# Evacuation adds in place, masks in the pooling stage, the two-quarter chunk's down groups whole, and quarter 7 of FFN 0 by eight products

## The chip, the cores and the metric

The kernel runs on one core of one Trainium2 chip. TensorE (PE) multiplies into PSUM; its weight loads are shown apart as PEld. VectorE (DVE) and ScalarE (ACT) do the elementwise work, GpSimd (POOL) and SyncE (SP) mostly issue transfers. The metric is the device time of one execution in microseconds, as the median of the runs.

## The reference

A trunk of two layers over 256 tokens of width 2048. Layer 0 mixes by causal pooling, layer 1 by dilated attention; each is followed by a gated feed-forward part (FFN) with a causal convolution of width 3, and each of the four sums is normalised. The FFN is where the change acts most:

```python
def conv_ffn(h, w_up, conv_w, conv_b, w_down):
    S = h.shape[1]
    u = h @ w_up
    up = jnp.pad(u, ((0, 0), (CONV_WIDTH - 1, 0), (0, 0)))
    c = conv_b + up[:, 0:S] * conv_w[0]
    for j in range(1, CONV_WIDTH):
        c = c + up[:, j:j + S] * conv_w[j]
    gate, val = jnp.split(c, 2, axis=-1)
    return (jax.nn.silu(gate) * val) @ w_down
...
        h = layer_norm(DEEPNORM_ALPHA * h + mix, ln1_g[i], ln1_b[i])
        ff = conv_ffn(h, ffn_w_up[i], ffn_conv_w[i], ffn_conv_b[i], ffn_w_down[i])
        h = layer_norm(DEEPNORM_ALPHA * h + ff, ln2_g[i], ln2_b[i])
```

The inner width is 5504 = 43 blocks of 128. In attention the scores are masked by which of the three dilated branches see a pair of positions, and weighted by how many do.

## The kernel before

Every weight is float32 and is multiplied as two float32r parts, a rounded high part (`wh`, cast by ScalarE) and the rest (`wl`, subtracted by VectorE), so that a product is three matmuls: high by high, low by high, high by low.

The program is one list of **units**. A unit is a block of weights of up to 512 x 512 with its load into a raw buffer (three in rotation, on SP's queue), its split into `wh` and `wl` (four in rotation), its matmuls, and what follows them. `run_units` writes them out in order: before unit i it issues loads up to unit i + 5 and splits up to unit i + 3, and behind its matmuls come the callbacks due (`later(n, fn)`: n units on), then the unit's own evacuation. Every engine works in the order written.

An FFN runs in eleven **quarters** of 512 inner columns (the last has three blocks, 384). `up(q)` gives quarter q's four gate units and four value units, 32 matmul steps each (24 in the last); their sums are evacuated (`evac`) from PSUM into a tile `u`, convolved (`conv`), and multiplied to `g`. The down product of the inner quarters is done in four **chunks**, of quarters 0 to 2, 3 to 5, 6 and 7, and 8 to 10. For each chunk `down(n)` gives four groups, one for each 512 output columns, of one item for each quarter. An item is either a plain unit (`go_t`: 24 matmuls of 512 columns, which is eight half-size products) or a **7-product** pair of units (`mk_seven`, kinds "a" and "b": 18 and 24 matmuls of 256 columns, seven half-size products). The latter needs sums and differences of the weights, formed in the raw buffer itself by `split_sums` (three VectorE steps more than a plain split, with the raw buffer held until kind "b" is split), and of the tokens, formed by `left_sums` when the quarter's `g` is ready, in borrowed buffers named by `sets`. `sevens` says which quarters do which column groups so. A group's sums lie in four PSUM banks (`t0`, `t1`, `s2`, `s3`); `early_post` and `tm_post` add them to the token-major residual `HT`, three transfers by POOL among them. In FFN 0 the third chunk is the last by tokens: three units behind each of its groups, `to_features` turns that residual back to feature-major by a VectorE transpose and 16 moves on SP's queue.

The groups of one chunk are laid among the up units of the next quarters by `weave`. With three items to a group there is one item behind each up unit but the first; with two items there is one before the first and one before the third up unit. Quarter 9's `g` is made only behind the last group of the two-quarter chunk (`free[9]`), since it takes a buffer that the group still reads; in FFN 1 its 7-product operands follow.

`evac` copies the second half of a PSUM bank with ScalarE to a tile of a ring of three (`ut`), and VectorE adds the first half to it into `u`; attention's `qk_post` does the same with a ring of two, `norm_evac` works likewise for the first group of a stage. The two mask tiles (`cnt`, `negm`) are made at the start of attention by `masks`, in that same ring.

Of the kernel before, what the change touches and what calls it, by code (L numbers as in the profile page):

```python
# [17 lines left out]
T = 256  # L18
# [14 lines left out]
def trunk(ctx: ExitStack, tc: tile.TileContext, x, pool_w_in, pool_w_grp, pool_scale, pool_w_out,  # L33
# [269 lines left out]
    inv = const.tile([P, 1, 16], F32, name="inv")  # L303

# [134 lines left out]
    def norm_evac(ps, nb, tmp, dst):  # L439
# [108 lines left out]
    def ffn(lay):  # L548
# [17 lines left out]
        def evac(ps, nb, mode):  # L566
            fp = pools["ffn"]
            u = pads()

            def tmp():  # L570
                return fp.tile([P, T], F32, name="ut", tag="t1", bufs=3)

            if mode == "x":
                norm_evac(ps, nb, tmp, lambda m: u[:, m, 2:])
                return u
            for m in range(nb):
                t = tmp()
                A.copy(t, ps[m][:, T:])  # L578
                V.tensor_tensor(u[:, m, 2:], ps[m][:, :T], t, OP.add)  # L579
# [155 lines left out]
        def down(n, last):  # L735
            qs = range(*chunks[n])
# [224 lines left out]
    def qk_post(nm, hq):  # L961
# [3 lines left out]
        def evac(ps):  # L965
# [4 lines left out]
            def tmp():  # L970
                return ap.tile([P, T], F32, name="qt", tag="t1", bufs=2)

            if hq == 0 and nm == "k":
                norm_evac(ps, 4, tmp, lambda m: o[:, m, :])
# [13 lines left out]
    def scores(hq, ms):  # L988
        ap = pools["attn"]
        for m in ms:  # L990
# [7 lines left out]
            sf, nf, cf = (t.rearrange("p a b -> p (a b)") for t in (s, ST["negm"], ST["cnt"]))  # L998
# [9 lines left out]
        for m in ms:  # L1008
            s, mx, _ = pr[hq, m]
            sf, cf = (t.rearrange("p a b -> p (a b)") for t in (s, ST["cnt"]))  # L1010
# [101 lines left out]
    with tc.tile_pool(name="pool", bufs=1) as pp:  # L1112
# [36 lines left out]

        later(2, lambda: late_consts(0))  # L1150
# [7 lines left out]
    with tc.tile_pool(name="attn", bufs=1) as ap:  # L1158
        pools["attn"] = ap
        for nm in ("cnt", "negm"):  # L1160
            ST[nm] = ap.tile([P, 3, P], F32, name=nm)

        def masks(i):
            two = ap.tile([P, 2, P], F32, name="dist", tag="t1", bufs=2)
# [54 lines left out]
```

## Time and profile before

| | us |
|---|---|
| median of 3 runs (lowest, highest) | 2051.32 (2048.59, 2051.43) |
| the profiled execution | 2051.56 |
| its span | 2049.8 |
| FFN 0, third chunk with the up groups of quarters 9 and 10 | 745.4 to 870.8 |
| FFN 0, last chunk begins | 870.8 |
| attention begins | 938.8 |
| FFN 1, third chunk with the up groups of quarters 9 and 10 | 1853.0 to 1974.1 |
| FFN 1, last chunk begins | 1974.1 |

Times in the views are microseconds from the span's start. A row of the waits reads: engine, tile and line that waited, the releaser, the total, the number of times, the longest. A row of the stretches reads: the stretch, its length, then for PE, PEld, DVE, ACT and POOL the busy time with the number of instructions, then the granted clock of PE, the share of DMA time and GB/s. In a timeline row stand the start, the length, engine, line and operation, and in brackets the idle time before it with its releaser.

### The profile page before, as it was taken

Reading aid. Unit: us, or ns where it says so; the run is one execution under the profiler, and the core shown is the slowest. Engines: PE = TensorE matmul, PEld = TensorE weight load, DVE = VectorE, ACT = ScalarE, POOL = GpSimd, SP = SyncE. Lnnn points to the kernel's source line nnn. Section 1 sums busy time; section 2 is a strip of 40 time slices with the busy share of each in tenths; the row PEclk is TensorE's granted clock in tenths of the full one; section 3 lists DMA queues with packets and bytes.
Section 4 is the critical chain, followed back from the end, with each engine's and each line's share of the span. In section 5 each row is a group of like instructions: output and inputs, shape, how many; then the busy total and the mean of one; then the engine's idle time right before and its main releaser. Section 6 shows DMA issues by size and latency. Waiting matters only on the chain. (4 is left out here: it accounts for less than half of the span.)

```text
span 2049.8 us, 31251 instructions
## 1 busy us (share of the span) xinstructions
PE 2025.5 (99%) x12532; PEld 1809.4 (88%) x12532; DVE 1684.2 (82%) x2010; ACT 1259.6 (61%) x1691; POOL 74.9 (4%) x111
## 2 busy tenths in 40 slices
PE   9999999999999999999999999999999999999998
PEld 8899988899899989889888888998899988889987
DVE  6759876998889898889856657787889888989989
ACT  6545687666756686657544444477666677667663
POOL 2000000000000101000000000000001000100000
PEclk9999999999999999999999999999999999999999
DMA  8655467667656657775566554557666756666565
GB/s 263 213 190 186 169 211 202 191 194 235 196 190 201 202 190 210 211 231 170 167 218 191 173 180 165 185 185 221 187 199 185 227 181 208 205 216 197 184 206 185
DMA packets 278305, 405.92 MB, mean 198 GB/s; under 512 B 80414, under 2 KB 95668, under 8 KB 277904
## 3 DMA queue, kind: packets, MB, share of 16 engines
q1 hardware_dynamic: 266144, 389.72, 57.5%
q0 software_dynamic: 11584, 13.55, 4.4%
q8 instruction: 98, 1.61, 0.3%
q10 hardware_dynamic: 432, 0.66, 0.1%
q14 instruction: 47, 0.39, 0.1%
HBM read 380.01 MB, written 2.10 MB: 186 GB/s over the span
## 5 line engine op out<-in xcount | busy, mean ns | idle before, releaser
L165 PE MATMUL acc<-xc,wh 128*128 128x512 f32 x3264 | 1152.8, 396 | 1.2 <-DVE o L1064 1.2
L166 PE MATMUL acc<-xc,wl 128*128 128x256 f32 x3264 | 917.3, 281 | 5.3 <-DVE wl L83 5.1
L83 DVE TENSOR_TENSOR wl<-raw,wh 128x2048 fp32r<-128x2048 f32 (+2 forms) x318 | 687.5, 2168 | 259.1 <-ACT wh L82 258.7
L165 PEld LDWEIGHTS acc<-xc,wh 128*128 128x128 f32 x3264 | 615.9, 189 | 144.4 <-DVE o L1064 1.9
L82 ACT CAST wh<-raw 128x2048 fp32r<-128x2048 f32 (+2 forms) x318 | 573.7, 1810 | 201.2 <-PE acc L165 108.4
L166 PEld LDWEIGHTS acc<-xc,wl 128*128 128x128 f32 x3264 | 615.4, 189 | 9.2 <-DVE wl L83 8.5
L96 ACT CAST wh<-raw 128x1024 fp32r<-128x1024 f32 x116 | 121.9, 1053 | 156.8 <-DVE raw L107 133.4
L97 DVE TENSOR_TENSOR wl<-raw,wh 128x1024 fp32r<-128x1024 f32 x116 | 138.4, 1221 | 0.0
L103 ACT CAST wh<-raw 128x1024 fp32r<-128x1024 f32 x116 | 90.7, 832 | 35.6 <-DMA raw<-in_ffn_w_down_dram 21.3
L106 DVE TENSOR_TENSOR wl<-raw,wh 128x1024 fp32r<-128x1024 f32 x116 | 105.7, 952 | 2.6 <-ACT wh L103 2.2
L587 ACT ACTIVATE c<-u,cv 128x256 f32<-128x256 f32 x172 | 89.5, 593 | 24.6 <-DVE f L650 8.5
L578 ACT COPY ut<-acc 128x256 f32<-128x256 f32 x164 | 53.1, 372 | 81.6 <-DVE u L579 58.6
L228 PE MATMUL t<-wl,g 128*128 128x256 f32 x344 | 97.0, 282 | 0.0
L227 PE MATMUL t<-wh,g 128*128 128x256 f32 x344 | 97.0, 282 | 0.0
L229 PE MATMUL t<-wh,g 128*128 128x256 f32 x344 | 96.7, 281 | 0.0
L228 PE MATMUL s<-wl,xs 128*128 128x256 f32 x308 | 86.9, 282 | 3.8 <-DVE wl L97 3.8
L229 PE MATMUL s<-wh,xs 128*128 128x256 f32 x308 | 86.4, 280 | 0.0
L227 PE MATMUL s<-wh,xs 128*128 128x256 f32 x308 | 86.3, 280 | 0.0
L271 POOL DMA_DIRECT2D ht<-w x24 | 20.3, 847 | 1770.6 <-ACT wh L103 1034.8
L592 ACT ACTIVATE a<-u,cv 128x256 f32<-128x256 f32 x172 | 73.6, 501 | 12.3 <-DVE g L660 6.5
L592 ACT ACTIVATE u<-u,cv 128x256 f32<-128x256 f32 x172 | 73.5, 500 | 0.0
L109 DVE TENSOR_TENSOR raw<-raw 128x1024 f32<-128x1024 f32 x58 | 71.0, 1225 | 2.0
(278 smaller groups left out, 3433.8 us busy)
## 6 DMA issues: line engine op xcount, KB each, us to landing
raw<-in_ffn_w_up_dram SPq DMA_DIRECT2D x160, 1024.0 KB, 4.9
raw<-in_ffn_w_down_dram SPq DMA_DIRECT2D x80, 1024.0 KB, 5.1
raw<-in_pool_w_out_dram SPq DMA_DIRECT2D x16, 1024.0 KB, 5.0
raw<-in_shared_w_k_dram SPq DMA_DIRECT2D x16, 1024.0 KB, 5.1
raw<-in_attn_w_q_dram SPq DMA_DIRECT2D x16, 1024.0 KB, 5.4
raw<-in_shared_w_v_dram SPq DMA_DIRECT2D x16, 1024.0 KB, 5.6
raw<-in_attn_w_o_dram SPq DMA_DIRECT2D x16, 1024.0 KB, 5.0
raw<-in_pool_w_in_dram SPq DMA_DIRECT2D x12, 1024.0 KB, 5.5
```

Of the source, the lines that this page charges most:

```text
L82: A.copy(wh[i][:, s], r[:, s])
L83: V.tensor_tensor(wl[i][:, s], r[:, s], wh[i][:, s].bitcast(F32), OP.subtract)
L96: A.copy(h[:, :, n], r[:, :, n])
L97: V.tensor_tensor(l[:, :, n], r[:, :, n], h[:, :, n].bitcast(F32), OP.subtract)
L103: A.copy(h[:, k, n], r[:, k, n])
L106: V.tensor_tensor(l[:, k, n], r[:, k, n], h[:, k, n].bitcast(F32), OP.subtract)
L165: PE.matmul(ps[m], h[:, k, c], q[:, k, :, :T], start=st, stop=False)
L166: PE.matmul(ps[m][:, :T], l[:, k, c], q[:, k, 0, :T], start=False, stop=sp and not shifted)
L227: PE.matmul(to, xh, h[:, k, n], start=opens and kk == 0, stop=False)
L228: PE.matmul(to, xh, l[:, k, n], start=False, stop=False)
L229: PE.matmul(to, xl, h[:, k, n], start=False, stop=ends and kk == 1)
L592: A.activation(to[:, m, :], u[:, m, i:i + T], AF.Copy, scale=cv[:, i, j:j + 1])
```

## The change

It has four parts.

- Evacuation: ScalarE copies straight into the target tile, and VectorE adds the other half of the bank onto it there. The rings `ut` and `qt` are gone, in `evac`, `qk_post` and `norm_evac`.
- Masks: `cnt` and `negm` become constants of the whole program and are made in the pooling stage, behind units 11 and 12, in buffers that the normalisation uses later.
- Two-quarter chunk, both FFNs: a group's items stand together, behind a whole up group.
- FFN 0, quarter 7: plain units in place of 7-product pairs, in the order 7, 6; it has no left sums.

```diff
+    cnt = const.tile([P, 3, P], F32, name="cnt")
+    negm = const.tile([P, 3, P], F32, name="negm")
...
-    def norm_evac(ps, nb, tmp, dst):
+    def norm_evac(ps, nb, dst):
...
-            ts = [(m, tmp()) for m in range(m0, min(nb, m0 + 2))]
+            ts = [(m, dst(m)) for m in range(m0, min(nb, m0 + 2))]
...
-                A.activation(dst(m), t, AF.Identity, scale=-1.0, bias=wgb[:, m, 1:2])
+                A.activation(t, t, AF.Identity, scale=-1.0, bias=wgb[:, m, 1:2])
...
-        sets = {0: "C", 1: "A", 2: "B", 3: "C", 4: "A", 5: "B", 6: "A", 7: "BC"[1 - lay], 9: "A"}
+        sets = {0: "C", 1: "A", 2: "B", 3: "C", 4: "A", 5: "B", 6: "A", 7: "B", 9: "A"}
         if lay == 1:
             sevens[9] = (0, 2)
+        else:
+            del sevens[7]
...
             for m in range(nb):
-                t = tmp()
-                A.copy(t, ps[m][:, T:])
-                V.tensor_tensor(u[:, m, 2:], ps[m][:, :T], t, OP.add)
+                A.copy(u[:, m, 2:], ps[m][:, T:])
+                V.tensor_tensor(u[:, m, 2:], u[:, m, 2:], ps[m][:, :T], OP.add)
...
-            qs = range(*chunks[n])
+            qs = (7, 6) if n == 2 and lay == 0 else range(*chunks[n])
...
         d = down(2, False)
-        for us in up(8):
+        for us, ks in zip(up(8) + up(9) + up(10), [()] + d + [()]):
             units.extend(us)
-        for us, ks in zip(up(9) + up(10), d):
-            free[9] = weave(us, ks)[-1]
+            units.extend(ks)
+        free[9] = len(units) - 5
...
             for m in range(4):
-                    t = tmp()
-                    A.copy(t, ps[m][:, T:])
-                    V.tensor_tensor(o[:, m, :], ps[m][:, :T], t, OP.add)
+                    A.copy(o[:, m, :], ps[m][:, T:])
+                    V.tensor_tensor(o[:, m, :], o[:, m, :], ps[m][:, :T], OP.add)
...
         def masks(i):
-            two = ap.tile([P, 2, P], F32, name="dist", tag="t1", bufs=2)
-            dist, fm = two[:, 0], two[:, 1]
+            both = lnp.tile([P, 4, T], F32, name="dist", tag="sq")
+            dist, fm = (both[:, j, :P] for j in range(2))
+            two = lnp.tile([P, 2, T], I32, name="idist", tag="fold2")
+            idist, im = two[:, 0, :P], two[:, 1, :P]
...
         for i in range(2):
-            later(7 + i, lambda i=i: masks(i))
+            later(9 + i, lambda i=i: masks(i))
```

The order of the loads shows the new place of the groups. On SP's queue, in FFN 1, the last two groups of the two-quarter chunk before (`raw400` is the number of the unit that the load serves; down loads are the pairs, up loads of 384 columns belong to quarter 10):

```order
L72 DMA raw396_18240<-in_ffn_w_down_dram 128x4x512
L72 DMA raw398_18323<-in_ffn_w_up_dram 128x4x384
L72 DMA raw399_18364<-in_ffn_w_up_dram 128x4x384
L72 DMA raw400_18405<-in_ffn_w_down_dram 128x4x512
L72 DMA raw402_18457<-in_ffn_w_up_dram 128x4x384
L72 DMA raw403_18505<-in_ffn_w_up_dram 128x4x384
L72 DMA raw404_18537<-in_ffn_w_down_dram 128x4x512
L72 DMA raw406_18608<-in_ffn_w_up_dram 128x4x384
L72 DMA raw407_18648<-in_ffn_w_up_dram 128x4x384
L72 DMA raw408_18687<-in_ffn_w_down_dram 128x4x512
```

The same place of the changed program:

```order
L72 DMA raw394_18003<-in_ffn_w_up_dram 128x4x384
L72 DMA raw395_18039<-in_ffn_w_up_dram 128x4x384
L72 DMA raw396_18069<-in_ffn_w_down_dram 128x4x512
L72 DMA raw398_18143<-in_ffn_w_down_dram 128x4x512
L72 DMA raw400_18208<-in_ffn_w_up_dram 128x4x384
L72 DMA raw401_18251<-in_ffn_w_up_dram 128x4x384
L72 DMA raw402_18285<-in_ffn_w_up_dram 128x4x384
L72 DMA raw403_18320<-in_ffn_w_up_dram 128x4x384
L72 DMA raw404_18348<-in_ffn_w_down_dram 128x4x512
```

Before, every third load is a down load, three loads behind the one before it; now two stand together, then four up loads, and `raw404` already belongs to the last chunk, with two more up units between it and the last pair.

The same queue in FFN 0, before, with the moves of `to_features` (`h<-hb`):

```order
L72 DMA raw172_7917<-in_ffn_w_down_dram 128x4x512
L72 DMA raw174_8002<-in_ffn_w_up_dram 128x4x384
L804 DMA h_8037<-hb_7995 32x8x32 x6
L72 DMA raw175_8050<-in_ffn_w_up_dram 128x4x384
L804 DMA h_8037<-hb_7995 32x8x32 x5
L72 DMA raw176_8096<-in_ffn_w_down_dram 128x4x512
L804 DMA h_8037<-hb_7995 32x8x32 x5
L72 DMA raw178_8153<-in_ffn_w_up_dram 128x4x384
```

And in the changed program, where `raw173` is quarter 7's plain unit and `raw174` quarter 6's pair:

```order
L72 DMA raw169_7755<-in_ffn_w_up_dram 128x4x384
L72 DMA raw170_7800<-in_ffn_w_up_dram 128x4x384
L803 DMA h_7840<-hb_7798 32x8x32 x6
L72 DMA raw171_7857<-in_ffn_w_up_dram 128x4x384
L803 DMA h_7840<-hb_7798 32x8x32 x5
L72 DMA raw172_7901<-in_ffn_w_up_dram 128x4x384
L803 DMA h_7840<-hb_7798 32x8x32 x5
L72 DMA raw173_7936<-in_ffn_w_down_dram 128x4x512
L72 DMA raw174_7985<-in_ffn_w_down_dram 128x4x512
```

The moves stood around the second down load of a pair; now they stand among the group's last two up loads and ahead of the next group's plain load.

The third place is VectorE at the end of FFN 1's third chunk. Before, quarter 9's low part (`g`) and its left sums (`f`) come behind the split of `wl408`, the first unit of the last chunk:

```order
L83 TENSOR_TENSOR wl407_18721<-raw407_18648,wh407_18720 128x1536
L83 TENSOR_TENSOR wl408_18743<-raw408_18687,wh408_18742 128x2048
L286 TENSOR_TENSOR g_18770<-c_17996,g_18770 128x4x256
L646 TENSOR_TENSOR f_18777<-c_17996 128x256
L647 TENSOR_TENSOR f_18777<-f_18777,c_17996 128x256
L648 TENSOR_TENSOR f_18777<-c_17996 128x256
L650 TENSOR_TENSOR f_18777<-c_17996,f_18777 128x256
```

In the changed program they come behind the third of the last four up units, `wl402`; the first unit of the last chunk is now 404:

```order
L592 TENSOR_TENSOR c_18281<-c_18281,u_18243 128x768
L83 TENSOR_TENSOR wl402_18351<-raw402_18285,wh402_18350 128x1536
L286 TENSOR_TENSOR g_18378<-c_17680,g_18378 128x4x256
L645 TENSOR_TENSOR f_18385<-c_17680 128x256
L646 TENSOR_TENSOR f_18385<-f_18385,c_17680 128x256
L647 TENSOR_TENSOR f_18385<-c_17680 128x256
L649 TENSOR_TENSOR f_18385<-c_17680,f_18385 128x256
```

Two splits of short up units, 403 and with it the unit before the last chunk's first, have moved from ahead of quarter 9's operands to behind them.

More of the change, by code (lines that the diff above doesn't have):

```diff
@@ L997, in scores @@
             s = two[:, m % 2]
-            sf, nf, cf = (t.rearrange("p a b -> p (a b)") for t in (s, ST["negm"], ST["cnt"]))
+            sf, nf, cf = (t.rearrange("p a b -> p (a b)") for t in (s, negm, cnt))
             V.scalar_tensor_tensor(sf, ps[:, :3 * P], scale, nf, op0=OP.mult, op1=OP.add)
@@ L1009, in scores @@
             s, mx, _ = pr[hq, m]
-            sf, cf = (t.rearrange("p a b -> p (a b)") for t in (s, ST["cnt"]))
+            sf, cf = (t.rearrange("p a b -> p (a b)") for t in (s, cnt))
             for t, sl in parts:
```

45 lines of the change are left out of this document (18 added, 27 removed).

## The prediction

> **What bounds the kernel now.** The first view is the page: it says which engine is full.
>
> ```profile
> span 2049.8 us, 31251 instructions
> PE 2025.5 (99%) x12532; PEld 1809.4 (88%) x12532; DVE 1684.2 (82%) x2010; ACT 1259.6 (61%) x1691; POOL 74.9 (4%) x111
> ```
>
> TensorE is busy 99% of the span, so a change can only pay by issuing fewer matmuls or by taking away the few places where PE waits. The second view is the list of PE's waits, which names the releasers.
>
> ```profile
> PE acc L166 <- DVE wl L83: 5.1, 8, 2.0
> PE s L228 <- DVE wl L97: 3.8, 4, 1.5
> PE t L229 <- DVE xs3Q L660: 1.9, 1, 1.9
> ...
> PE acc L165 <- DVE o L1064: 1.2, 1, 1.2
> PE acc L165 <- DVE w L829: 1.1, 1, 1.1
> ...
> PE acc L165 <- DVE u L835: 0.7, 1, 0.7
> ```
>
> All of these wait for VectorE. The sums are too small, though: the end of a matmul is modelled, the records overlap, and the head of every stall hides behind the matmul before it. The third view therefore compares stretches that issue the same matmuls. The bounds of each are starts of units; the count in brackets includes the matmuls that overlap an edge.
>
> ```profile
> 745.45:778.46 33.01, 32.64 (x215) 29.50 (x213) 31.38 (x34) 25.86 (x36) 0.78 (x2) 1.00 0.57 191
> 810.84:841.22 30.38, 27.29 (x182) 24.66 (x181) 27.74 (x33) 18.85 (x30) 2.58 (x3) 1.00 0.77 208
> 841.22:870.78 29.56, 27.59 (x182) 24.72 (x181) 22.71 (x24) 17.87 (x25) 2.59 (x3) 1.00 0.75 210
> 870.78:879.15 8.37, 6.53 (x34) 4.94 (x33) 8.23 (x12) 4.43 (x5) 2.58 (x3) 1.00 0.81 228
> 879.15:884.80 5.65, 5.65 (x35) 4.92 (x34) 3.18 (x6) 5.30 (x10) 0.00 (x0) 1.00 1.02 333
> 1853.03:1885.75 32.72, 32.68 (x215) 29.56 (x213) 31.09 (x34) 25.58 (x36) 0.76 (x2) 1.00 0.56 193
> 1885.75:1918.15 32.40, 32.40 (x215) 29.55 (x213) 30.14 (x34) 22.12 (x31) 4.41 (x6) 1.00 0.68 203
> 1918.15:1945.04 26.89, 26.89 (x183) 24.65 (x182) 23.36 (x28) 17.39 (x26) 0.00 (x0) 1.00 0.65 207
> 1945.04:1974.10 29.06, 27.68 (x183) 24.77 (x181) 23.48 (x25) 19.25 (x26) 2.59 (x3) 1.00 0.70 219
> 1974.10:1988.92 14.82, 12.61 (x69) 11.14 (x67) 14.60 (x25) 8.84 (x16) 2.58 (x3) 0.88 0.50 126
> 2008.42:2018.96 10.54, 10.54 (x68) 9.49 (x66) 10.40 (x13) 6.20 (x5) 0.00 (x0) 1.00 0.34 108
> ```
>
> A group of the two-quarter chunk with three-block up units (two pairs of 7-product units and four up units, 180 matmuls) takes 26.89 us when nothing is late. In FFN 0 the two such groups take 30.38 and 29.56, a loss of 3.49 + 2.67 = 6.2 us, and the first group of full up units takes 33.01 where 32.40 is the calm length, 0.6. The first unit of the last FFN 0 chunk takes 8.37 where its twin takes 5.65: 2.7 us. In FFN 1 the groups lose 0.32 + 2.17 = 2.5 us, and the opening of its last chunk (a plain unit and a 7-product pair, 66 matmuls) takes 14.82 against 10.54: 4.3 us. Together **16.3 us** of stalls in the stages whose order is changed.
>
> Why the groups stall is read from the VectorE timeline of the late FFN 1 group and from the load queue.
>
> ```profile
> 1948.57 0.37 SPq L72 DMA_DIRECT2D raw<-in_ffn_w_down_dram  x1
> ...
> 1955.15 0.69 DVE L104 TENSOR_TENSOR raw<-raw 128x512 f32<-128x512 f32 x1 [2.26 <-DMA raw<-in_ffn_w_down_dram]
> 1956.24 1.83 DVE L106 TENSOR_TENSOR wl<-raw,wh 128x1024 fp32r<-128x1024 f32 x2 [0.40 <-ACT wh L103]
> 1958.10 0.69 DVE L107 TENSOR_TENSOR raw<-raw 128x512 f32<-128x512 f32 x1
> 1958.83 1.22 DVE L109 TENSOR_TENSOR raw<-raw 128x1024 f32<-128x1024 f32 x1
> 1959.97 0.95 DVE L593 TENSOR_TENSOR c<-c,a 128x768 f32<-128x768 f32 x1
> 1960.84 2.35 DVE L97 TENSOR_TENSOR wl<-raw,wh 128x1024 fp32r<-128x1024 f32 x2
> ...
> 1963.98 1.75 DVE L83 TENSOR_TENSOR wl<-raw,wh 128x1536 fp32r<-128x1536 f32 x1
> ...
> SPq L72 <- DVE wl L97: 421.1, 54, 10.2
> ```
>
> The load of the second pair's weights leaves at 1948.57, VectorE idles 2.26 us for it at 1955, and the pair's second half is split only from 1960.84, when PE is at that unit. The load left late because there are three raw buffers and the woven order is 7-product, up, up: each 7-product load takes the buffer of the 7-product load before it, which is held through all five split steps (L104 to L97). The queue's own waits say so: 54 loads waited for an L97. VectorE is not short of time here (23.48 us busy of 29.06); it is late.
>
> **The change, part by part.**
>
> *Eight products in place of seven.* A plain unit is 24 matmuls of 512 columns, a 7-product pair 42 of 256:
>
> ```profile
> 1974.10:1979.68 5.58, 5.58 (x27) 4.52 (x26) 5.42 (x12) 1.24 (x3) 1.70 (x3) 1.00 0.44 144
> 1853.03:1857.99 4.96, 4.96 (x44) 4.96 (x43) 4.96 (x7) 4.07 (x8) 0.00 (x0) 1.00 0.55 194
> ```
>
> 5.58 - 4.96 = 0.62 us of PE per column group, four groups: **+2.5 us**, on the engine that sets the end. VectorE gets back 0.69 + 1.83 + 0.69 + 1.22 + 2.35 = 6.8 us per pair and pays 2.3 for a plain split (the 512-column form of the 1.75 us row above), plus 0.3 for a full-width add of t1: some 4 us per group, 16 in all, and the left sums of quarter 7 fall away.
>
> *Groups whole.* With loads in the order 7, 6, up, up, up, up (6 then 7 in FFN 1) the three buffers turn differently: the first load of a group takes the buffer of the second of the four up units before it, and the second that of the third, both freed after one short split. A buffer held by a 7-product pair now goes to the second or third up unit behind it, which has slack. Walked through for the tightest place, the last group of FFN 1, from the start of up group 10's gate units (PE: short up unit (26.89 - 2 x 4.96) / 4 = 4.24, so 17.0; the group 9.9, to 26.9; four up units, to 43.9; plain unit, to 49.4). A split can start three units ahead of its unit, when PE frees the weight buffer. Split 7a may start at 12.7 and ends at 17.1; the evacuation of the gate ends at 18.3; split 7b ends at 20.6 and PE wants it at 24.1. Then three up splits of 1.75 (two convolution adds of 0.95 between them), quarter 9's four left sums and its low part (2.6 by the rows below), the group's own evacuation (2.6) and the fourth up split end near 34.4, wanted at 39.6. The plain split ends near 38, the two halves of quarter 9's pair near 42.4 and 44.7, wanted at 49.4 and 51.5. The smallest slack is 3.5 us, and no PE wait is left. In FFN 0 the group owes VectorE 4 us less.
>
> *The opening of the last chunk.* In FFN 1 quarter 9's own operands are made only behind the last group, which now ends four up units before the chunk in place of two:
>
> ```profile
> 1970.33 2.29 DVE L83 TENSOR_TENSOR wl<-raw,wh 128x2048 fp32r<-128x2048 f32 x1 [2.24 <-ACT wh L82]
> 1972.54 1.22 DVE L286 TENSOR_TENSOR g<-c,g 128x1024 fp32r<-128x1024 f32 x1
> 1973.68 0.42 DVE L646 TENSOR_TENSOR f<-c 128x256 f32<-128x256 f32 x1
> ...
> 1982.96 0.42 DVE L660 TENSOR_TENSOR xs3Q<-f,xs3S 128x256 fp32r<-128x256 f32 x1
> ```
>
> They are begun at 1972.5 and end at 1983.4, while PE waits. Two up units more are 8.5 us of PE time ahead of them, against a wait of 4.3. In FFN 0 the same shift frees the product banks that the 8.37 us unit waits for (L829 and L835 in PE's waits). What becomes late next is quarter 10's value chain, which still starts at the last up unit.
>
> ```profile
> 1983.10 0.91 ACT L578 COPY ut<-acc 128x256 f32<-128x256 f32 x3
> ...
> 1991.05 0.96 DVE L684 TENSOR_TENSOR c<-c 128x768 f32<-128x768 f32 x1
> ```
>
> In FFN 1 its copies began at 1983.10 and its product ended at 1992.0; with the cast and the low part behind that, my estimate is 13 us, and it has 49.4 + 4.96 + 5.6 - 43.9 = 16.
>
> *What follows each group.* The 16 small moves of FFN 0's turn to features keep their number and stand between other loads:
>
> ```profile
> 852.46 3.87 SPq L804 DMA_DIRECT2D h<-hb  x6
> ```
>
> 0.65 us of queue each, 10.3 per group. They now stand ahead of the last two up loads and the next plain load, whose splits have over 5 us in the walk. I charge nothing; if that cover is gone, one load is late by up to 3.9 us per group.
>
> *Evacuation in place and masks.* The copy loses its ring of three:
>
> ```profile
> ACT ut L578 <- DVE u L579: 58.6, 27, 3.8
> ...
> L1176 DVE SCALAR_TENSOR_TENSOR cnt<-dist,cnt x4: 292/293/295, 987.9 to 995.4; 128x128 f32<-128x128 f32 x4
> 82.78 2.29 DVE L83 TENSOR_TENSOR wl<-raw,wh 128x2048 fp32r<-128x2048 f32 x1 [3.28 <-ACT wh L82]
> ```
>
> ScalarE loses 58.6 us of waiting, but it is 61% busy and PE's waits name it nowhere in these stages. The add keeps its form and time. Two of the 164 copies now begin with a wait on VectorE for the buffer of u itself; behind it stand weight casts with three units of lead. The masks are ten VectorE steps of 0.22 to 0.29 us, 2.4 us twice. They move into the pooling stage, where VectorE idles 3.28 us before the split at 82.78; without that cover they would cost 2.4 us each. In the attention stage they ended 40 us before PE's one wait there (o L1064, 1.2 us), so between 0 and 1.2 is gained. I take zero for both edits, with -1.2 to +2.4.
>
> **The sum.** Of 16.3 us I let a fifth stay (3.3), because the walk leaves out loads that land late and ScalarE's share: 13.0 gained, 2.5 paid, 10.5 net. The profiled execution took 2051.56 (span 2049.8 and 1.8 around it), 0.24 above the median of the three runs, so 2051.56 - 10.5 = 2041.1. All stalls gone gives 2037.8, half of them 2045.9.
>
> **The rivals.**
>
> *The loads are the limit.* In FFN 0 the late groups moved 208 and 210 GB/s; to take 27.5 us in place of 30 they need 230. Against it: one unit moved 333. If so, the two groups stay at 30 us and absorb their own share of the price (1.2), and only four fifths of 0.6 + 2.7 + 2.5 + 4.3 are gained: 2051.6 - 8.1 + 1.2 = 2044.7.
>
> *Only FFN 0 gains.* If VectorE is simply full in FFN 1 (31.09 of 32.72 us in one group), its 6.8 us stay and four fifths of FFN 0's 9.5 go: 2051.6 - 7.6 + 2.5 = 2046.5.
>
> *The burst starves PE (slower).* In FFN 1 the two 7-product pairs now stand back to back: 2 x 6.8 = 13.6 us of VectorE for 9.9 us of PE, 3.7 us short. The walk covers it with 3.5 us of slack; if VectorE comes later than the walk by more than that, each further microsecond is PE's, in four groups. With the whole shortage paid, 4 x 3.7 = 14.8 in place of 2.5, the tail unchanged, FFN 0 as forecast: 2051.6 + 2.5 - 7.6 + 12.3 = 2059; half the shortage gives 2051. The Trainium skill (Perfetto Trace Analysis, Optimization Strategy) says that regimes bound by different engines may gain from being interleaved; the change takes interleaving away, so that rule stands on this rival's side. The trace so far speaks against it: the interleaved order is the one that stalls.
>
> *The waits move and only the price counts (slower).* PE is at 99%, the work of VectorE in FFN 1 is the same, and a wait removed may come back three units later: 2051.6 + 2.5 = 2054. The Trainium skill (Perfetto Trace Analysis, Identifying the Most-Contended Engine) has one improve the engine with the highest occupancy first; here that is PE, and the change adds to it. Against it stands the calm group of 26.89 us with 3.5 us of VectorE idle.
>
> **How the numbers follow.** The forecast of 2041 gets 0.68, the load limit 0.14, gain in FFN 0 alone 0.07, the burst 0.06, the price alone 0.05. The range runs from 2037 (all stalls gone, and most of the attention wait) to 2047.5 (the first two rivals); outside are the slower cases and their neighbours. A difference of 0.2%, 4.1 us, is about what this measurement can tell from none: faster means under 2047.2. Nearly all of the forecast, the load limit and half of FFN 0 alone lie there: 0.84. Within 0.2%: 0.09, the rest of these and the milder ends of the slower rivals. Slower: 0.07.
>
> **What would show it.** Right: groups of FFN 1 at 26.9 and 32.4 us, those of FFN 0 at about 33.0 and 27.5; the opening of FFN 1's last chunk near 10.6; PE's wait for xs3Q gone; the load queue's wait for L97 far under 421 us. Wrong: stalls at the second pair of FFN 1's groups (the burst), VectorE idle for loads in FFN 0 with DMA shares of 0.8 or more (the load limit), a new wait at quarter 10's first use, or 7-product loads that still land less than three units ahead.

## The result, and the profile after

| | before | changed |
|---|---|---|
| median, us | 2051.32 | 2030.07 |
| lowest, highest (5 runs each) | 2048.59, 2053.28 | 2029.58, 2031.27 |
| profiled execution, its span | 2051.56, 2049.8 | 2031.27, 2029.5 |

The ratio is 0.9899 with an interval of 0.9885 to 0.9914: the change takes 21 us, twice the 10.5 that were forecast, and the time lies below the range. The page of the changed kernel, its first lines:

```profile
span 2029.5 us, 31025 instructions
...
PE 2021.9 (100%) x12460; PEld 1807.1 (89%) x12460; DVE 1664.9 (82%) x1979; ACT 1253.3 (62%) x1676; POOL 75.0 (4%) x111
```

And the whole list of PE's waits of half a microsecond and more:

```profile
PE acc L168 <- ACT wh L82: 1.3, 1, 1.3
PE warm L1093 <- DVE one L1089: 1.1, 1, 1.1
PE xT L518 <- DMA xin<-in_x_dram: 0.9, 1, 0.9
```

PE's busy time fell by only 3.6 us and its idle time from 24.3 to 7.6. Every wait that the prediction showed is gone; the three that are left end within the first 10 us, up to the matmuls of the first unit. The stretches that answer to those of before, again bounded by unit starts:

```profile
636.60:744.83 108.23, 108.23 (x703) 98.19 (x702) 97.96 (x106) 72.98 (x98) 5.17 (x6) 1.00 0.69 218
744.83:865.59 120.76, 120.76 (x715) 106.50 (x714) 95.96 (x97) 74.76 (x98) 10.36 (x12) 1.00 0.76 220
777.83:810.83 33.00, 33.00 (x197) 29.07 (x196) 25.61 (x26) 20.60 (x27) 2.59 (x3) 1.00 0.77 210
838.21:865.59 27.38, 27.38 (x165) 24.18 (x164) 20.75 (x22) 15.92 (x19) 2.59 (x3) 1.00 0.87 247
865.59:871.21 5.62, 5.62 (x35) 4.91 (x34) 3.29 (x5) 3.61 (x6) 0.00 (x0) 1.00 0.67 193
1873.77:1906.16 32.39, 32.39 (x215) 29.55 (x214) 30.14 (x36) 22.25 (x30) 2.59 (x3) 1.00 0.67 209
1932.95:1959.74 26.79, 26.79 (x183) 24.63 (x182) 25.82 (x35) 18.48 (x25) 2.59 (x3) 1.00 0.72 223
1959.74:1970.30 10.56, 10.56 (x69) 9.47 (x68) 9.47 (x12) 9.77 (x16) 0.00 (x0) 1.00 0.65 225
```

Where the second number equals the first, PE had no gap at all. That now holds in every row: the groups of FFN 1 take 32.39 and 26.79, those of FFN 0 33.00 and 27.38 (0.6 more, the eight products' price), and the openings of the last chunks 5.62 and 10.56 against 8.37 and 14.82. The first row is a stretch that the prediction never looked at, the second chunk of FFN 0, with three items to a group. Before, the same 703 matmuls took longer:

```profile
635.29:745.45 110.16, 109.13 (x703) 98.25 (x702) 97.61 (x109) 70.11 (x96) 6.75 (x8) 1.00 0.65 206
```

Neither its order nor its products were changed, yet it is 1.9 us shorter and without a gap. That points at the evacuation, which the experiments take by itself.

### The profile page after: what moved, and what is told of

The parts are those of the page before. It is cut to its first block, busy times and chain, and to the rows that moved or that the text cites. A ratio compares the mean times of both kernels' runs of the same rounds, so it can differ in the third digit from the quotient of the medians.

```text
span 2029.5 us, 31025 instructions
## 1 busy us (share of the span) xinstructions
PE 2021.9 (100%) x12460; PEld 1807.1 (89%) x12460; DVE 1664.9 (82%) x1979; ACT 1253.3 (62%) x1676; POOL 75.0 (4%) x111
## 4 chain that ended last, share of the span: by engine, by line
PE 99%; DMA 0%; SPq 0%; DVE 0%; ACT 0%; issue 0%; DVEq 0%
PE acc L165 43%; PE acc L166 22%; PE t L238 3%; PE t L240 3%; PE t L239 3%; PE acc L169 3%; PE acc L170 3%; PE acc L168 3%; PE s L228 3%; PE s L227 2%; PE s L229 2%; PE t L228 2%; PE t L227 2%; PE t L229 2%; PE s L989 0%; PE o L1056 0%
## 5 line engine op out<-in xcount | busy, mean ns | idle before, releaser
L83 DVE TENSOR_TENSOR wl<-raw,wh 128x2048 fp32r<-128x2048 f32 (+2 forms) x322 | 697.0, 2169 | 251.7 <-ACT wh L82 248.6
L82 ACT CAST wh<-raw 128x2048 fp32r<-128x2048 f32 (+2 forms) x322 | 582.0, 1812 | 221.4 <-PE acc L165 120.3
L96 ACT CAST wh<-raw 128x1024 fp32r<-128x1024 f32 x108 | 112.9, 1053 | 149.0 <-DVE raw L107 123.1
L97 DVE TENSOR_TENSOR wl<-raw,wh 128x1024 fp32r<-128x1024 f32 x108 | 129.1, 1221 | 1.4 <-ACT wh L96 1.4
L103 ACT CAST wh<-raw 128x1024 fp32r<-128x1024 f32 x108 | 84.5, 832 | 48.5 <-PE acc L165 33.8
L106 DVE TENSOR_TENSOR wl<-raw,wh 128x1024 fp32r<-128x1024 f32 x108 | 98.3, 951 | 1.7 <-ACT wh L103 1.4
L228 PE MATMUL t<-wl,g 128*128 128x256 f32 x320 | 89.8, 281 | 0.0
L227 PE MATMUL t<-wh,g 128*128 128x256 f32 x320 | 89.8, 281 | 0.0
L229 PE MATMUL t<-wh,g 128*128 128x256 f32 x320 | 89.7, 280 | 0.0
L271 POOL DMA_DIRECT2D ht<-w x24 | 20.3, 847 | 1809.2 <-ACT wh L103 771.9
L577 ACT COPY u<-acc 128x256 f32<-128x256 f32 x164 | 54.7, 373 | 51.5 <-PE acc L166 51.4
L229 PE MATMUL s<-wh,xs 128*128 128x256 f32 x284 | 79.2, 279 | 0.0
L228 PE MATMUL s<-wl,xs 128*128 128x256 f32 x284 | 79.2, 279 | 0.0
L227 PE MATMUL s<-wh,xs 128*128 128x256 f32 x284 | 79.2, 279 | 0.0
L238 PE MATMUL t<-wh,g 128*128 128x512 f32 (+1 forms) x179 | 68.2, 381 | 0.0
```

Of the source, the lines that this page charges most:

```text
L82: A.copy(wh[i][:, s], r[:, s])
L83: V.tensor_tensor(wl[i][:, s], r[:, s], wh[i][:, s].bitcast(F32), OP.subtract)
L96: A.copy(h[:, :, n], r[:, :, n])
L97: V.tensor_tensor(l[:, :, n], r[:, :, n], h[:, :, n].bitcast(F32), OP.subtract)
L106: V.tensor_tensor(l[:, k, n], r[:, k, n], h[:, k, n].bitcast(F32), OP.subtract)
L227: PE.matmul(to, xh, h[:, k, n], start=opens and kk == 0, stop=False)
```

## The experiments

In each run one part is done alone, left out, or replaced. A diff is against the kernel before, unless another is named.

**The parts alone.** The evacuation in place, everywhere:

```diff
...
-                t = tmp()
-                A.copy(t, ps[m][:, T:])
-                V.tensor_tensor(u[:, m, 2:], ps[m][:, :T], t, OP.add)
+                A.copy(u[:, m, 2:], ps[m][:, T:])
+                V.tensor_tensor(u[:, m, 2:], u[:, m, 2:], ps[m][:, :T], OP.add)
...
```

> Before with the in-place evacuation alone (FFN, attention, norm). Theory A (ring): in the ring of three, ScalarE's fourth copy waits for VectorE's first add, a weight cast stands behind that copy, and VectorE then idles for that cast; without the ring the stalls of the three-quarter chunk (1.9 us in FFN 0, 1.3 in FFN 1) and of attention (1.2) go, and some of the two-quarter chunk's: 5 to 9 us less than before, 2042 to 2046. Theory B (as forecast): ScalarE's waits hide nothing, 2050 to 2052, and those 4.5 us come from the new order of the groups.

2038.93 us, ratio 0.9936 (0.9923 to 0.9948): 13 us, more than any other part alone, and 3 us below the numbers of theory A, which had the mechanism but gave it too little.

The groups whole, with seven products and the old ring:

```diff
-        for us in up(8):
+        for us, ks in zip(up(8) + up(9) + up(10), [()] + d + [()]):
             units.extend(us)
-        for us, ks in zip(up(9) + up(10), d):
-            free[9] = weave(us, ks)[-1]
+            units.extend(ks)
+        free[9] = len(units) - 5
```

> Before with the two-quarter chunk's groups whole, seven products kept in both FFNs, ring and masks as before. If the raw buffers' turn is the cause of the 16.3 us of stalls, the order alone takes most of them: 2035 to 2039, with the stalls of the three-quarter chunk still there. If two pairs back to back starve PE (the burst), FFN 0, where VectorE also turns the residual, stalls at the second pair: 2045 or more.

2052.78 us, ratio 1.0002 (0.9993 to 1.001): nothing, where I had put most of the gain; the number is that of the burst.

Eight products for quarter 7, in the woven order:

```diff
+        else:
+            del sevens[7]
...
-            qs = range(*chunks[n])
+            qs = (7, 6) if n == 2 and lay == 0 else range(*chunks[n])
```

> Before with quarter 7 of FFN 0 by plain units, in the order 7, 6, still woven; nothing else. Price on PE 2.5 us. If VectorE's 4 us per group and the buffer held by quarter 7's pair caused FFN 0's stalls, 7 or 8 of the 9.5 us go: 2045 to 2047. If the price alone counts: 2053 to 2054.

2043.78 us, ratio 0.9961 (0.9949 to 0.9974): 1.2 us below the lower end of what was expected.

A milder order, the second pair of a group one up unit behind the first:

```diff
-                if len(items) == 2 and i % 2 == 0:
-                    put(items[i // 2])
+                if len(items) == 2 and i < 2:
+                    put(items[i])
```

> Before with one change of order: the second pair of a two-quarter group stands behind the first up unit in place of the second (pair, up, pair, up, up, up). The pairs are still apart, but a pair's load no longer takes the buffer of the pair before it. If the buffers' turn is the cause: as far as the whole groups, within 2 us of that run. If it is the whole group itself (four or more calm up units behind it): little gained, 2048 or more.

2043.34 us, ratio 0.9956 (0.9942 to 0.9969): 9 us better than whole groups, so neither of the two expectations holds. It frees the openings as they do (21.10 us in FFN 0 against 23.85, 40.67 in FFN 1 against 44.86), but in FFN 0 the shift stage behind the opening takes 14.81 in place of 11.97, so nothing is won there. Its group stages take 122.19 and 119.44 us, less than before where whole groups take more (the table below).

**The change less one part.** Without the evacuation in place, and without the masks' move, which needs the room that the rings gave back:

```diff
+        else:
+            del sevens[7]
...
-            qs = range(*chunks[n])
+            qs = (7, 6) if n == 2 and lay == 0 else range(*chunks[n])
...
-            free[9] = weave(us, ks)[-1]
+            units.extend(ks)
...
```

> The change without the evacuation in place and without the masks' move: whole groups and eight products on the old ring of three. Theory A (the ring's wait is what the burst of a whole group runs into, and only the evacuation in place takes it away): the parts add as the single runs did by stage, FFN 0's groups -4.6 (eight products) and +2.2 (whole groups), its opening -2.8, FFN 1's groups +3.6, its opening -4.3, together about -6, so 2044 to 2047 us. Rival B (order and products carry the change; the evacuation gives only what lies outside the re-ordered stages, some 8 us): 2036 to 2040 us.

2043.09 us, ratio 0.9956 (0.9944 to 0.9969): 13.0 us above the changed kernel, 1 below theory A's numbers and 3 above the rival's.

Quarter 7 at seven products again (against the changed kernel):

```diff
...
-        else:
-            del sevens[7]
...
-            qs = (7, 6) if n == 2 and lay == 0 else range(*chunks[n])
+            qs = range(*chunks[n])
```

> The changed kernel with quarter 7 of FFN 0 at seven products again; all else as changed. Theory A (with the evacuation in place VectorE keeps ahead even with the weight sums of seven products): four times 0.62 us of matmuls less and no stall in their place, 2027 to 2028.5 us. Rival (the eight products pay, because they spare VectorE the sums of that quarter's weights): FFN 0's group stage takes 1 to 4 us of stalls for the 2.5 us of matmuls saved, 2029 to 2033 us.

2035.85 us, ratio 0.9923 (0.991 to 0.9937). Theory A's number missed here; the loss is larger even than the rival's.

The woven order again (against the changed kernel):

```diff
-        for us, ks in zip(up(8) + up(9) + up(10), [()] + d + [()]):
+        for us in up(8):
             units.extend(us)
-            units.extend(ks)
-        free[9] = len(units) - 5
+        for us, ks in zip(up(9) + up(10), d):
+            free[9] = weave(us, ks)[-1]
```

> The changed kernel with the pairs of products of the two-quarter chunk woven between the up units again, as before; evacuation in place, masks and eight products as changed. Theory A (order and evacuation are of use together, and each by its own place): the opening of FFN 1's last chunk waits again as it did with the evacuation alone, 43.9 against 40.6 us, and FFN 0's does not, since eight products alone took that wait away: 2033 to 2034 us. Rival (with the evacuation in place the order is of no more account): 2029.5 to 2031 us.

2035.47 us, ratio 0.9925 (0.9912 to 0.9939), 1.5 us above theory A's numbers, which had left out the end of the kernel (last row of the table).

The masks at the start of attention again (against the changed kernel):

```diff
...
-            cn = cnt[:, i, :]
+            cn = ST["cnt"][:, i, :]
...
-            later(9 + i, lambda i=i: masks(i))
+            later(7 + i, lambda i=i: masks(i))
```

> The changed kernel with the masks made at the start of attention, as before. Theory A (the masks cost nothing in either place, and the 1.3 us that attention's head gained came with the evacuation alone, whose masks were late as well): 2029.5 to 2031 us, attention's head at 47.8 us. Rival (the late masks hold up VectorE at attention's start): 2031 to 2034 us.

2030.67 us (2030.27 to 2032.02), ratio 0.9898 (0.9885 to 0.9912): the same as with all parts.

Where each part works is seen stage by stage. The lengths are differences of unit starts in the profiled executions, in us; the "end" runs from the last twelve matmuls to the end of the span. Eight products put 2.5 us into the second row. The profiled execution of whole groups alone is the fastest of its eleven runs (2048.13 us), so its column shows less loss than its median.

| stage | before | changed | evac. alone | whole alone | eight alone | less evac. | less eight | less whole |
|---|---|---|---|---|---|---|---|---|
| FFN 0, second chunk | 110.16 | 108.23 | 108.23 | 109.76 | 109.76 | 109.72 | 108.23 | 108.23 |
| FFN 0, two-quarter groups | 125.36 | 120.76 | 120.67 | 127.53 | 120.73 | 120.76 | 123.99 | 120.73 |
| FFN 0, last chunk's opening, shift | 35.82 | 31.50 | 35.78 | 33.68 | 31.57 | 31.63 | 36.25 | 31.56 |
| attention, second head | 49.09 | 47.82 | 47.83 | 49.04 | 49.89 | 50.11 | 47.81 | 47.76 |
| FFN 1, second chunk | 121.08 | 119.68 | 119.55 | 120.90 | 120.62 | 120.62 | 119.49 | 119.71 |
| FFN 1, two-quarter groups | 121.07 | 118.36 | 118.40 | 124.67 | 120.61 | 126.53 | 118.37 | 118.43 |
| FFN 1, last chunk's opening | 44.86 | 40.64 | 43.89 | 40.57 | 44.76 | 40.64 | 40.57 | 43.94 |
| end | 11.12 | 9.50 | 11.33 | 9.63 | 11.22 | 9.50 | 9.68 | 11.06 |

The whole order does what was forecast at FFN 1's opening (4.3 us alone, 3.3 where the evacuation is in place as well) and 1.6 us at the end besides, but behind the old ring it costs the groups themselves 2.2 and 3.6 us. Three rows of the stretches of that kernel (groups of FFN 0, groups of FFN 1, opening), and a fourth for the last group of FFN 1 alone:

```profile
744.43:871.96 127.53, 121.54 (x787) 109.66 (x786) 115.31 (x127) 84.51 (x116) 10.35 (x12) 0.99 0.73 207
1851.89:1976.57 124.68, 121.01 (x787) 110.06 (x786) 114.69 (x133) 84.87 (x119) 10.35 (x12) 0.99 0.67 201
1976.57:2017.13 40.56, 40.56 (x219) 34.70 (x218) 38.47 (x45) 25.33 (x29) 0.00 (x0) 1.00 0.64 210
...
1949.76:1976.57 26.81, 26.81 (x183) 24.67 (x182) 25.73 (x34) 18.55 (x25) 2.58 (x3) 1.00 0.71 216
```

What the order loses, it loses in the groups with full up units. Group by group the whole order takes 38.77, 33.55, 26.77 and 28.45 us in FFN 0, against 33.01, 32.38, 30.38 and 29.56 before, and 37.35, 33.73, 26.79 and 26.80 in FFN 1, against 32.72, 32.40, 26.89 and 29.06. The late groups, on which the prediction rested, do gain.

Why the old ring hurts is seen at the first two-quarter group of FFN 1. With whole groups alone, ScalarE and VectorE in order of time (the last bracket is the idle time before the row and what ended it; PE began the second half of the second pair at 1859.83):

```profile
1854.70 0.90 ACT L578 COPY ut<-acc 128x256 f32<-128x256 f32 x3
1856.80 1.23 DVE L109 TENSOR_TENSOR raw<-raw 128x1024 f32<-128x1024 f32 x1
1857.96 0.41 DVE L579 TENSOR_TENSOR u<-acc,ut 128x256 f32<-128x256 f32 x1
1858.46 0.37 ACT L578 COPY ut<-acc 128x256 f32<-128x256 f32 x1 [2.86 <-DVE u L579]
1858.73 2.00 ACT L96 CAST wh<-raw 128x1024 fp32r<-128x1024 f32 x2
1859.81 2.36 DVE L97 TENSOR_TENSOR wl<-raw,wh 128x1024 fp32r<-128x1024 f32 x2 [0.45 <-ACT wh L96]
1864.52 2.29 DVE L83 TENSOR_TENSOR wl<-raw,wh 128x2048 fp32r<-128x2048 f32 x1 [2.34 <-ACT wh L82]
```

And the same place of the changed kernel, where PE began that half at 1848.44:

```profile
1841.55 0.38 ACT L577 COPY u<-acc 128x256 f32<-128x256 f32 x1 [1.03 <-PE acc L166]
1841.67 1.23 DVE L109 TENSOR_TENSOR raw<-raw 128x1024 f32<-128x1024 f32 x1
1841.82 2.15 ACT L96 CAST wh<-raw 128x1024 fp32r<-128x1024 f32 x2
1842.83 0.41 DVE L578 TENSOR_TENSOR u<-u,acc 128x256 f32<-128x256 f32 x1
1844.15 2.35 DVE L97 TENSOR_TENSOR wl<-raw,wh 128x1024 fp32r<-128x1024 f32 x2
1847.79 2.29 DVE L83 TENSOR_TENSOR wl<-raw,wh 128x2048 fp32r<-128x2048 f32 x1 [1.29 <-ACT wh L82]
```

A full up group has four blocks and the ring has three tiles. So the fourth copy waits for VectorE's first add, and that add stands in VectorE's program behind all of L104 to L109 of the next pair. Behind the waiting copy stands L96, the cast that VectorE needs for its L97, and behind that the cast for the next L83. Each engine waits for the other in turn: the copy 2.86 us, then VectorE 0.45 and 2.34. With the copy straight into `u` there is no such wait, the cast runs beside L109, and L97 starts 4.3 us ahead of PE's need in place of 0.0.

**The wait itself.** Two kernels tell the wait from other effects of writing in place. In the first only the fourth copy goes straight to `u`, and the first three keep the ring:

```diff
-                t = tmp()
+                t = tmp() if m < 3 else u[:, m, 2:]
```

> Before, with one thing changed: of the four copies of an FFN evacuation the first three keep the ring of three, the fourth goes straight to its place in u and is added to there, so that no copy waits for an add; attention and the normalising evacuation as before. Theory A (the wait of the fourth copy for the first add, with the weight cast behind it on ScalarE's queue, is the cost): nearly all of what the evacuation in place gave alone, less the 1 us it gave in attention, 2038.5 to 2042 us. Rival (in-place saves by what it does to memory or to the adds, not by the wait): 2049 to 2052 us.

2041.21 us, ratio 0.9947 (0.9935 to 0.996). In the second all is in place, except that blocks 0 and 3 share one tile, so that the fourth copy waits as before (against the evacuation alone):

```diff
-                A.copy(u[:, m, 2:], ps[m][:, T:])
-                V.tensor_tensor(u[:, m, 2:], u[:, m, 2:], ps[m][:, :T], OP.add)
+                t = u[:, m, 2:]
+                if m in (0, 3):
+                    t = pools["ffn"].tile([P, T], F32, name="ut", tag="t1", bufs=1)
+                A.copy(t, ps[m][:, T:])
+                V.tensor_tensor(u[:, m, 2:], ps[m][:, :T], t, OP.add)
```

> Evacuation in place everywhere except that blocks 0 and 3 of an FFN evacuation share one buffer, so that the fourth copy waits for the first add again. Theory A: the FFN stages stall as before the change and only attention keeps its gain, 2048 to 2052 us. Rival (not the wait): as with the evacuation in place alone, 2037 to 2040 us.

2049.74 us, ratio 0.999 (0.9982 to 0.9999). ScalarE's waits in that kernel show the wait of before (58.6 us, 27 times) back:

```profile
ACT ut L576 <- DVE u L577: 59.4, 27, 3.8
```

One wait is taken away and 10 us go; it is put back and they return, but for the 1.3 us in attention, whose evacuation stays in place in that kernel (47.83 us for the second head). The ring's wait is the cause of those 10 us.

**What loads had to do with it.** My account of the group stalls was the late load of the second pair. With the evacuation alone the order of the loads is that of before. Its queue's waits, and its VectorE at the place of the late FFN 1 group that the prediction quoted:

```profile
SPq L72 <- DVE wl L97: 419.1, 54, 10.2
```

```profile
1942.45 0.69 DVE L104 TENSOR_TENSOR raw<-raw 128x512 f32<-128x512 f32 x1 [2.26 <-DMA raw<-in_ffn_w_down_dram]
...
1948.14 2.36 DVE L97 TENSOR_TENSOR wl<-raw,wh 128x1024 fp32r<-128x1024 f32 x2
```

The load is as late for VectorE as before, to the hundredth (2.26 us of idle time), and 54 loads still wait for an L97. But PE comes to the half that this L97 serves at 1950.95 here, 2.8 us behind its start, where before it came at 1960.92, 0.1 behind the start at 1960.84. The group stages of this kernel:

```profile
743.85:864.52 120.67, 118.72 (x787) 108.23 (x785) 105.61 (x117) 80.33 (x109) 7.77 (x9) 1.00 0.72 210
1843.86:1962.26 118.40, 118.40 (x787) 108.43 (x786) 104.66 (x117) 82.25 (x112) 7.77 (x9) 1.00 0.66 206
```

In FFN 1 not a gap is left, with the same late load. So the late load alone does not make PE wait. The lead of VectorE tells the rest: by the starts of L97 and of the half it serves, it was 3.7 us at the first pair of FFN 1's first group before and 8.1 here, and 0.1 against 2.8 at the late group. Quarter 10's up units have three blocks, which fit the ring, so the loss came along from the full units before. On the way to the late group the lead falls in both kernels, by 3.6 and 5.3 us.

Nor was the load innocent. With whole groups alone, VectorE does not idle for a load in that last group at all, its lead is 2.7 us, and the group takes 26.80 us with the old ring still there. In this place two losses of lead had to meet, the ring's and the late load's; taking either away is enough.

**Looking for less.** With seven products the changed kernel loses 5.7 us in the groups of FFN 0 and 4.7 in the shift behind the opening, for 2.5 us of matmuls (the rows show the groups and the shift):

```profile
742.24:866.22 123.98, 119.94 (x787) 108.45 (x786) 109.30 (x122) 81.74 (x109) 10.35 (x12) 1.00 0.75 208
887.33:902.47 15.14, 12.10 (x64) 10.38 (x63) 12.50 (x16) 6.59 (x6) 0.00 (x0) 0.89 0.74 253
```

VectorE has 109.3 us of work there for 118.3 us of PE without gaps (120.76 less 2.5), with `to_features` between; with eight products (row of the changed kernel above) it has 95.96. It falls behind over the stage: by unit starts the first two groups with seven products have no stall of note, the last two have 1.6 and 4.0 us. Two more kernels start from that. The first spreads the pairs, with seven products (against the changed kernel, `weave` as in the milder order above):

```diff
...
-        else:
-            del sevens[7]
...
-                if len(items) == 2 and i % 2 == 0:
-                    put(items[i // 2])
+                if len(items) == 2 and i < 2:
+                    put(items[i])
...
-            qs = (7, 6) if n == 2 and lay == 0 else range(*chunks[n])
+            qs = range(*chunks[n])
...
-            units.extend(ks)
-        free[9] = len(units) - 5
+        for us, ks in zip(up(9) + up(10), d):
+            free[9] = weave(us, ks)[-1]
```

> The changed kernel with seven products for quarter 7 and with the second pair of each group one up unit after the first, in place of whole groups. Theory (in FFN 0 VectorE has too little time for the weight sums of both quarters when they come at once, and a spread order gives it some): FFN 0's groups at 118.5 to 122 us against 124.0 with whole groups and seven products, 2029 to 2033 us. Rival (the sum of VectorE's work in that stage decides, whatever the order): 2034 to 2036 us.

2030.99 us, ratio 0.9899 (0.9886 to 0.9913). FFN 0's groups fall to 118.69 us, with hardly a stall left, but the shift stage takes 15.83 in place of 10.42, with one wait of PE:

```profile
PE shift L364 <- DVE S L347: 3.6, 1, 3.6
```

The wait is 3.6 of the 5.4 us; the granted clock of PE, one half for 3.41 us right behind it, is 1.7 more (the last section). Whole groups with seven products had this late shift too (15.14), so the spread order mends the groups and not the shift. The second has seven products for quarter 7 in the first two groups and eight in the last two (against the changed kernel, `sets` as before):

```diff
-            del sevens[7]
+            sevens[7] = (0, 1)
```

> The changed kernel with quarter 7 of FFN 0 at seven products in the first two groups of the two-quarter chunk and at eight in the last two, where the run with seven products everywhere had its stalls. Theory (VectorE falls behind over the stage, and is late only in the last two groups): 1.24 us of matmuls less and no new stall, 2028.5 to 2029.5 us. Rival (the sums of the gated values that seven products need, and the splits of the weight sums in the first groups, leave VectorE as late): 2031 to 2034 us.

2028.69 us (2028.31 to 2029.17), ratio 0.9887 (0.9874 to 0.9901): all runs lie below all runs of the changed kernel. Both stages, groups and opening with the shift, are without a gap:

```profile
743.17:862.85 119.68, 119.68 (x751) 107.41 (x750) 104.58 (x112) 80.02 (x104) 10.35 (x12) 1.00 0.78 226
862.85:894.35 31.50, 31.50 (x184) 27.60 (x183) 24.03 (x26) 16.39 (x21) 0.00 (x0) 1.00 0.73 224
```

That is 1.1 us less than the changed kernel in the groups, near the 1.24 of two pairs, and the best time of the study.

## Why the prediction was right and wrong

**Right: which stalls would go, and the price.** Of the stalls in the re-ordered stages, forecast at 16.3 us, the groups of FFN 0 lost 125.36 - 120.76 + 2.5 = 7.1, the unit that opens its last chunk 2.8, the groups of FFN 1 2.7 and the opening there 4.2: 16.8, all of them. (Of the 4.2, 1.7 had been no wait but PE at half its clock; the prediction's own row shows it as a granted clock of 0.88.) Which part would take them was wrong, as follows. The price of 0.62 us per group was met: 27.38 against 26.79 us.

**Wrong, the step that failed: "I take zero for both edits".** For the masks zero was right. The evacuation in place was worth 13 us, alone (2052.08 to 2038.93 within its runs) and as the part left out (2043.09 to 2030.07), where "-1.2 to +2.4" was allowed. The other parts without it come within 2 us of the forecast of 2041.1, but that is luck: FFN 1's groups take 5.5 us more there, where the forecast had 2.5 us of stalls mostly gone. The reason given was that ScalarE "is 61% busy and PE's waits name it nowhere in these stages". Both were true and neither mattered: ScalarE's 58.6 us of waiting did not stop PE, it stopped casts that VectorE's splits were waiting for, and PE's waits then named VectorE. That weight casts stand behind a waiting copy was seen, but only for the two copies that the change makes wait, and "three units of lead" was supposed for them; behind the old ring's wait that lead was gone, as in the group shown above (0.0 us). The wait was quoted in the prediction and read as harmless.

**Half right: "why the groups stall".** The turn of the raw buffers was one of two conditions. In the late groups, the ones that the prediction read, the order alone takes 4.7 of 6.2 us in FFN 0 and all in FFN 1; but so does the evacuation alone in FFN 1, with the load just as late. The walk was for the last group, and its "no PE wait is left" held there even with the old ring (26.80 us). In the groups with full up units, for which nothing was walked through, the same order makes things worse by itself, until the ring is gone. The Trainium skill (Perfetto Trace Analysis, Optimization Strategy) says that a gap that keeps repeating on the engine that should be full can mean too little memory for the next tile. The runs agree: the wait for a tile in a ring of three, with four blocks to go through it, was worth 10 us. Two rings showed waits, the raw buffers' and this one; the kernel with the fourth copy alone in place showed what the second is worth.

**The burst was real, by another way.** The rival that two pairs back to back starve PE, at 0.06, is what whole groups do behind the old ring: 2.2 and 3.6 us alone, 5.5 in FFN 1 in the kernel less the evacuation (1.7, 1.7 and 3.4 us of them by a granted clock of one half behind the waits). But VectorE was not short by its own work there, as that rival had it: the same pairs stand back to back in the changed kernel without a gap. It lost the time in the mutual waits. Where VectorE's own work does seem to be too much is FFN 0 with seven products and without the ring (123.99 us). The rule of the Trainium skill (Perfetto Trace Analysis, Optimization Strategy) that regimes may gain from being interleaved holds in both these places: the woven order is the faster by 2.2 and 3.6 us behind the ring, and the spread one by 5.3 in FFN 0 with seven products (118.69). In the changed kernel it does not hold: the woven order is the slower by 5.4 us, and its groups take the same time.

**Terms left out or mis-sized.** A fifth of the stalls was to stay, 3.3 us; nothing stayed, and they were 0.5 more than counted. Outside the re-ordered stages the evacuation gave 1.9 and 1.4 us in the two second chunks and 1.3 in attention (the upper end of 0 to 1.2 was for the masks, which had no part in it). Eight products gave 1.5 in the shift, where PE waits for VectorE's sums, and the whole order 1.6 at the end; I had priced neither. Against these stand 1.3 us more before FFN 0's second chunk (the last section) and 0.6 that builds up evenly, without a gap, over FFN 1's first quarters and first chunk. The kernels with eight products, in all or in two groups, have 0.4 to 0.7 of it in common; it stays unexplained. Together 10.5 + 0.5 + 3.3 + 4.6 + 3.1 - 1.9 = 20.1, and the span fell by 20.3.

**Parts that overlap.** In FFN 0's groups eight products alone take every stall away, with either order and with either evacuation; the evacuation alone takes 4.7 of 7.1. So no part has a share of its own there. In FFN 1's groups as a whole only the evacuation does it, at FFN 1's opening only a new order, whole or milder (the evacuation takes 1.0 there).

**What the signs said.** Of the marks named, those on lengths came true, and so did the end of PE's wait for xs3Q. The mark for the cause did not. The load queue's wait for L97 was to fall "far under 421 us":

```profile
SPq L72 <- DVE wl L97: 370.3, 49, 10.2
```

It fell by 51 us, and the 49 waits that are left stop nothing: the sum of this queue's waits does not tell whether PE stalls. The load limit's sign, a DMA share of 0.8 or more, came as well (0.87 and 247 GB/s in FFN 0's last group), but PE has no gap there, so that rival is out.

The kernel with only the fourth copy in place takes 122.87 us in FFN 0's groups where all in place takes 120.67; 1.7 of these 2.2 us are a granted clock of one half behind a wait (the last section). Left open: the other 0.5, and why attention's second head takes 0.8 to 1.0 us more in the two kernels with eight products and the old ring.

## What to carry to other kernels

When an engine that is far from full shows waits, look at what stands behind the waiting instruction on its queue before calling it cover: here a copy waiting for a ring tile held up the very casts that the engine it waited for needed next. A ring shorter than the burst that goes through it can couple two engines; count its tiles against the burst, and test by taking that one wait away before moving work about. And a move that concentrates work is to be priced with the lead that is there when it lands, alone and together with the other parts.

## What the runs showed of the hardware

A wait of PE can cost more than itself. In the fourteen profiled executions the granted clock of PE, else 1.00, fell to one half twelve times between the first 20 us and the last 5: for 3.41 us each, once for twice that. Each time it began during a wait of PE of 0.7 us or more, or within 1.5 us of its end. Half the clock for 3.41 us costs 1.7 us. Two such stretches, in FFN 1's opening before and in FFN 0's last two-quarter group with the fourth copy alone in place:

```profile
1984.90:1988.30 3.40, 3.40 (x18) 3.40 (x17) 3.40 (x6) 3.18 (x6) 0.00 (x0) 0.50 0.37 100
```

```profile
853.50:856.90 3.40, 3.40 (x16) 3.40 (x17) 3.40 (x3) 2.85 (x4) 0.00 (x0) 0.50 0.91 240
```

It does not follow every wait: FFN 0's groups before lost 6.8 us without it. The changed kernel has none of these, which is a part of what taking the waits away is worth.

The changed kernel and the one with seven products have the same instructions in the same order up to 636 us. In their profiled executions unit 1 began at 16.86 and 14.28 us, and the 2.6 us stayed to the end. Two things made them: PE waited 1.34 us for a weight's cast, until 9.5 us, in the first alone; and its granted clock was one half from 11.4 to 14.8 us there and 1.00 in the other. So the start alone spreads the total by more than some of these parts are worth, and stages have to be compared by their lengths. Against that, a stretch without stalls repeats: FFN 0's second chunk took 108.23 us in each of the eight profiled kernels whose fourth copy does not wait.
